# Forgetting attention scored in two products, and every attention score product made 128 rows deep

## The chip, the cores and the metric

The kernel runs on one core of a Trainium2 chip. TensorE (PE) multiplies matrices; its weight loads (PEld) are counted apart and can overlap the products. VectorE (DVE), ScalarE (ACT) and GpSimd (POOL) do the elementwise work, and SyncE (SP) starts the transfers. The metric is the device time of one execution in microseconds (us); lower is better.

## The reference, cut to what matters

The whole program is two transformer blocks in a row, in float32, over 512 tokens of 1024 features. The first block has a recurrence, a gating unit, attention over a memory and a feed-forward part; the change does not touch it. The second block has two layers; each mixes four branches of 8 heads of 64 features and then runs a feed-forward part. Two of the scores that the change touches:

```python
# forgetting attention: F is the running sum over tokens of log sigmoid(f_logit + f_bias), one per head
logits = einsum('bqhd,bshd->bhqs', q, k) * scale + Fq[..., None] - F[:, :, None, :]
p = softmax(where(causal, logits, neg)); out = einsum('bhqs,bshd->bqhd', p, v)

# selected attention: index scores choose the keys, each query then attends to its best 128
dots  = einsum('bqhd,bsd->bqhs', qi, ki)
score = einsum('bqhs,bqh->bqs', relu(dots), wb * w_scale)
```

Selected attention (after rotary embedding, one key head for 8 query heads) and sliding-window attention (rotary, two key heads, window 128) score queries against keys in the same way. The fourth branch, retention, has score products of its own, which stay as they are.

## The kernel before, in words

All float32 products are made from exact two-part splits: a value is a high part (type fp32r) plus a low part, and a weight product `psmm` runs three products per 128 features: high by high (L189), high by low (L190), low by high (L191). Each weight tile is loaded by SP, cast to its high part by ACT (L167), and its low part is made by POOL in this block (`sub`, L112). Three weight tiles of each part are held (`wp`, 3 buffers), and four PSUM banks for these products.

In block 2, `mix2` writes the work of a layer in this order: the rotary keys and index queries, the small natural parts `msc`, the selection (`select`), the sums' rows of the forgetting heads (`fox_rows`), then four forgetting pairs, four pairs of selected attention, the first branch's gates and products, the sliding windows, and so on. Attention itself is written as Python generators (`attend`). `pump(rate)` advances the first generator of a background list by that many steps between weight products, so that softmax work stands between weight products; `drain` runs one to its end. `select` sits in a second list, one step a pump: 3 steps of index scores, 8 steps of two rounds of maxima on DVE (`max`, `match_replace`), then the masks. A scheduler then orders each engine's instructions from this program order and its own model, and places tiles in free slots. A slot of 2 KiB a partition is taken with `g()`; there are 52 of them.

`attend` handles two heads (one pair) over four chunks of 128 queries. For each chunk and head it takes a PSUM bank (three of them, shared with the transposes), calls `score`, reduces the bank with the mask on DVE (L968), exponentiates on ACT (L124), scales on DVE (L982), and one chunk later transposes the probabilities (L995), copies them out (ACT, L998) and multiplies by the values (L1003), which takes 128 rows by 64 columns of the array. Causal chunks have 128, 256, 384 and 512 keys; sliding windows have 128 and then 256.

The score of a head needs the 64 features of q and k in high and low parts. For rotary heads, `stack_q` puts q's high part in one half of the partitions and its low part in the other, and `stack_k` holds the keys' high parts in both halves (`hh`) and the low parts in both halves (`ll`). L1089 multiplies all 128 rows of q by `hh`; L1090 multiplies the 64 rows of q's high part by the same rows of `ll`. The index scores of `select` do the same in L1106 and L1108. For forgetting heads, `fox_pair` builds a pair from the projections: `q` and `kk` per head, `kl` for both. L1074 is the 128-row product, L1075 the 64-row one with the keys' low parts, and L1077 a third with 4 rows, which adds `F_q - F_s` from the rows that `fox_rows` left in `fq` and `fk`: 128 partitions for four heads, each head's sums in the first four rows of a quarter, zeros in the rest.

Of the kernel before, what the change touches and what calls it, by code (L numbers as in the profile page):

```python
# [9 lines left out]
F32 = mybir.dt.float32  # L10
# [7 lines left out]
P = 128  # L18
# [27 lines left out]
# columns of the vector table  # L46
# [13 lines left out]
# columns of the constant table  # L60
# [11 lines left out]
class Builder:  # L72
# [14 lines left out]
    # ---- small helpers  # L87
# [8 lines left out]
    def g(self, dt=F32, n=None):  # L96
        """A slot of 2 KiB a partition that lives long."""
        x = self.gp.tile([P, S], dt, name=self.nm("g"), tag="g", bufs=NSLOT)
        return x if n is None else x[:, :n]
# [34 lines left out]
    def cload(self, name, i=0, long=False):  # L134
        """A constant of the table, brought in for a while."""
        x = self.g() if long else self.tmp()
        a = CST[name][0] + i * S
        self.nc.sync.dma_start(x, self.I["cst"][:, a:a + S])
        return x
# [23 lines left out]
    # ---- exact two-part splits  # L163
# [29 lines left out]
    def gemm_b(self, ps, w, x, start=True, stop=True, off=0):  # L193
        """out^T [features, tokens] += w^T x, w: (hi, lo) [P, len(x)*P], x: list of (hi, lo) tiles."""
        hi, lo = w
        for k, (xh, xl) in enumerate(x):
            a = off + k * P
            self.mm3(ps, hi[:, a:a + P], lo[:, a:a + P], xh, xl,
                     start and k == 0, stop and k == len(x) - 1)

    def gemm_a(self, src, x, ncol, units, ntok=S):
        """natural [tokens, ncol]: one bank per 128 tokens; src[u] is [P, kts*ncol]."""
# [14 lines left out]
    # ---- norms  # L217
    def rms_prep(self, xs, gname, n, gain=None):
        """Split x*g into hi/lo tiles; returns them with a call that leaves the per-token
        factors (row, column), to be made once a product has been set off."""  # L220
# [13 lines left out]
    def square_sum(self, acc, x, k, g=None):  # L234
        """acc += (x*g)^2, tile k of the features"""
# [21 lines left out]
    def to_row(self, rc, n):  # L257
        """[tokens, 1] columns to a row, the same on every partition."""
# [10 lines left out]
    # ---- the whole program  # L269
# [31 lines left out]
    # ================= block 1  # L301
    def mix1(self):
        nc, I = self.nc, self.I
        self.rate, self.lo_every = 1, LO_MIX1
        # the recurrence's inputs, by way of DRAM into blocks of 8 tokens
# [35 lines left out]
        # spatial gating  # L341
# [74 lines left out]
        # gated linear unit after the recurrence, then its projection  # L416
# [60 lines left out]
    def cmul(self, outr, outi, ar, ai, br, bi, shape, eng=None, neg_im=False):  # L477
        """Complex product; with neg_im, outi is minus the imaginary part."""
# [17 lines left out]
    def s5(self, xa_d):  # L496
        """Both directions of the recurrence, in 64 blocks of 8 tokens; partitions of the
        states: (direction, state). Leaves gelu(y), features on partitions, in self.ys5."""
# [10 lines left out]
        # powers of exp(lam * step)  # L509
# [23 lines left out]
        # b_bar = (lam_bar - 1) / lam * b  # L533
# [14 lines left out]
        # powers by position in a block: into the block's end state, and out of it  # L548
# [14 lines left out]
        # block inputs: [(s, c), g, j]  # L563
# [15 lines left out]
        # end-of-block states of each block alone  # L579
# [34 lines left out]
        # the recurrence over blocks  # L614
# [11 lines left out]
    def s5_out(self):  # L626
# [9 lines left out]
        for q in range(4):  # L636
            if q % 2 == 0:
# [36 lines left out]
                # lags -7..7 in DRAM; row s of the block reads lags -s..7-s  # L674
# [31 lines left out]
        # back to features on partitions: [(q, g, c) of one half, tokens]  # L706
# [42 lines left out]
    def xhead(self, h, q, o):  # L749
        """Softmax attention of one head over the memory."""  # L750
# [78 lines left out]
    def final1(self):  # L829
        """The norm that ends block 1 and the one that begins block 2, in one: products run on  # L830
        x*g1*g2, unscaled; the residual goes to DRAM."""
# [28 lines left out]
    # ================= block 2  # L860
# [16 lines left out]
    def finish(self, src, off, hs):  # L877
        """The last products, the last residual and the norm of the output, by token halves."""
# [36 lines left out]
    # ---- rotary embedding; a bank holds two heads, each as its two halves  # L915
# [15 lines left out]
    def stack_q(self, o):  # L931
        """A tile of each of two heads: high parts beside their 64 rows' low parts."""
# [7 lines left out]
    def stack_k(self, o):  # L940
        """Of each of two heads, the high parts twice and the low parts twice."""
# [9 lines left out]
    # ---- softmax attention of two heads over query chunks  # L951
    def attend(self, ys, pair, score, mask, init, value, blocks, sinks=None):
        """Generator; leaves the split output tile [2 heads x 64, tokens] in ys[pair]."""
# [59 lines left out]
    def fox_bias(self, l, msc):  # L1013
        """Running sums of log sigmoid(f + b), as rows for a product that adds F_q - F_s."""
# [12 lines left out]
    def fox_rows(self, f):  # L1027
# [3 lines left out]
        for hg in range(2):  # L1031
            # each head's sums in four rows of a quarter of the partitions
# [22 lines left out]
    def fox_pair(self, ys, pair, pq, pk, va):  # L1055
# [4 lines left out]
        q, kk, kl = [self.g(F32R) for _ in range(2)], [self.g(F32R) for _ in range(2)], self.g(F32R)  # L1060
        for i in range(2):
            r, o = slice(i * 64, i * 64 + 64), slice(64 - i * 64, 128 - i * 64)
            nc.scalar.copy(kk[i][r], tk[r])
            nc.scalar.copy(kk[i][o], tk[r])
            self.sub(kl[r], tk[r], kk[i][r].bitcast(F32))
            nc.scalar.copy(q[i][r], tq[r])
            self.sub(q[i][o], tq[r], q[i][r].bitcast(F32))

        def score(i, c, ps, k0, nk):
            r = slice(i * 64, i * 64 + 64)  # L1070
            h = 2 * pair + i
            qs = slice(c * P, (c + 1) * P)
            mm = nc.tensor.matmul
            mm(ps, q[i][:, qs], kk[i][:, k0:k0 + nk], start=True, stop=False)  # L1074
            mm(ps, q[i][r, qs], kl[r, k0:k0 + nk], start=False, stop=False)  # L1075
            r = slice(h % 4 * 32, h % 4 * 32 + 4)
            mm(ps, self.fq[h // 4][r, qs], self.fk[h // 4][r, k0:k0 + nk], start=False, stop=True)  # L1077
# [5 lines left out]
    def rope_pair(self, ys, pair, q, hh, ll, mask, init, value, blocks, sinks=None):  # L1083
        nc = self.nc

        def score(i, c, ps, k0, nk):
            qs = slice(c * P, (c + 1) * P)
            r = slice(i * 64, i * 64 + 64)
            nc.tensor.matmul(ps, q[i][:, qs], hh[:, k0:k0 + nk], start=True, stop=False)  # L1089
            nc.tensor.matmul(ps, q[i][r, qs], ll[r, k0:k0 + nk], start=False, stop=True)  # L1090
# [3 lines left out]
    def select(self, si, hh, ll, msc):  # L1094
        """Additive masks that leave the 128 best causal keys of each query."""
# [4 lines left out]
        for c in range(1, CHUNKS):  # L1100
            nk = (c + 1) * P
            sc = self.g(F32, nk)
            for h in range(4):
                ps = self.bank("sc")
                r = slice(h % 2 * 64, h % 2 * 64 + 64)
                nc.tensor.matmul(ps[:, :nk], si[h][:, c * P:(c + 1) * P], hh[:, :nk],  # L1106
                                 start=True, stop=False)
                nc.tensor.matmul(ps[:, :nk], si[h][r, c * P:(c + 1) * P], ll[r, :nk],  # L1108
                                 start=False, stop=True)
# [24 lines left out]
    def retain(self, ys, q, k, vc, sg):  # L1134
        """Retention and its head norm, chunk by chunk; q, k: four tiles [2 heads x 64, tokens]."""
# [10 lines left out]
        for c in range(CHUNKS):  # L1146
# [51 lines left out]
            # sums of each head for its norm  # L1198
# [37 lines left out]
    def branch(self, l, n, y, x, first, gens=(), lead=3):  # L1236
        """merged += 2 sigmoid(gate) * (y @ w_branch); the gates run ahead of the products
        with y, which gens may still be working on."""
# [29 lines left out]
    def out_proj(self, src, xd, m=None, scale=0.5, late=0):  # L1268
        """x += scale * (m @ w); merged, where no m is given, holds twice its value. The last
        tiles of m, late of them, may still be under way in the background."""  # L1270
# [29 lines left out]
    def mix2(self, l):  # L1300
# [16 lines left out]
        # keys of the single heads, the index queries, the small natural parts  # L1317
# [6 lines left out]
        # forgetting attention  # L1324
# [14 lines left out]
        # selected attention  # L1339
# [12 lines left out]
        # sliding windows  # L1352
# [16 lines left out]
        # retention  # L1369
# [80 lines left out]
# ---- the host: layout only  # L1450
def _pack_b(w, cols=None):
    """[K, N] -> [N/128, 128, K] blocks: stationary tiles of one output tile, all K."""
# [8 lines left out]
def _pack_b2(w):  # L1461
    """As _pack_b for K = 512, two output tiles to a unit."""
# [5 lines left out]
def _pack_a(w, cols, units):  # L1468
    """[K, N] -> [units, 128, K/128/units * N]: moving rows."""
# [45 lines left out]
def _layout(a):  # L1515
# [30 lines left out]
    # features of the recurrence as the kernel holds them: (half, quarter, group of four, channel)  # L1546
# [50 lines left out]
```

## Time and profile before

| | |
|---|---|
| median of 3 runs | 3202.38 us (3199.94 to 3208.05) |
| span of the profiled execution, first to last instruction | 3194.7 us |
| median less span | 7.7 us |
| TensorE busy | 98% of the span, 14986 products |
| weight loads, DVE, ACT, POOL busy | 79%, 59%, 42%, 30% |
| mean granted TensorE clock | 0.991 |

The page gives a span for the execution that was profiled and no other time of its own; what lies around the span is taken as the 7.7 us to the median. In rows of the trace, "128*128" is rows by columns of the array that a product or load uses, followed by the partitions and columns of what it streams; times are microseconds from the span's start. The ends of matmuls are modelled, so the step from one start to the next is read here and not their length.

### The profile page before, as it was taken

What the parts mean: (1) busy time and instruction counts of PE and PEld (TensorE: products, weight loads), DVE (VectorE), ACT (ScalarE), POOL (GpSimd) and SP (SyncE); (2) the same over time, 40 slices, a digit from 0 to 9 for tenths busy, and PEclk for the clock granted to TensorE, in tenths of its full rate; (3) what the DMA queues carried; (4) which work ended last, traced back from release to release, by engine and by line L of the source; (5) the groups of instructions that cost most, each with busy time, mean ns of one, the idle gap of its engine ahead of it and who ended that gap; (6) DMA issues with size and microseconds to landing.
All of it is one profiled execution on the core that took longest, in us unless ns stands there. A gap on an engine that the chain in (4) does not pass through costs nothing.

```text
span 3194.7 us, 39292 instructions
## 1 busy us (share of the span) xinstructions
PE 3122.7 (98%) x14986; PEld 2508.8 (79%) x14986; DVE 1876.0 (59%) x3423; ACT 1332.8 (42%) x2230; POOL 966.8 (30%) x578
## 2 busy tenths in 40 slices
PE   8998999999998999999999999999999999999998
PEld 6877878888887776777888888877777778888887
DVE  7898554455447685444456666548645454565575
ACT  5523343322225455545234333355455352343343
POOL 4234242211005332344454000053232545610011
PEclk9999999999999999999999999999999999999999
DMA  4224342323323211122223323332111222323322
GB/s 157 75 77 107 91 158 93 99 89 97 106 84 112 83 66 40 64 72 80 76 86 119 99 92 101 96 121 67 60 53 53 83 80 75 119 94 99 96 92 83
DMA packets 98076, 287.12 MB, mean 90 GB/s; under 512 B 11984, under 2 KB 20432, under 8 KB 97888
## 3 DMA queue, kind: packets, MB, share of 16 engines
q1 hardware_dynamic: 97888, 284.61, 27.9%
q8 instruction: 118, 1.93, 0.2%
q14 instruction: 70, 0.57, 0.1%
HBM read 274.64 MB, written 9.93 MB: 89 GB/s over the span
## 4 chain that ended last, share of the span: by engine, by line
PE 89%; DVE 6%; issue 2%; DMA 1%; POOL 1%; ACT 1%; SPq 0%; DVEq 0%; POOLq 0%; ACTq 0%
PE psmm L189 25%; PE psmm L191 25%; PE psmm L190 25%; PE pspv L1003 2%; DVE tmp L112 2%; PE pssc L995 2%; PE pssc L1090 1%; PE pssc L1089 1%; PE pssc L1075 1%; PE pssc L1077 1%; DVE tmp L1215 1%; DVE g L112 1%; PE pssc L1074 1%; POOL lo L112 1%; DVE s5t L112 0%
## 5 line engine op out<-in xcount | busy, mean ns | idle before, releaser
L191 PE MATMUL psmm<-g,lo 128*128 128x512 f32 (+1 forms) x3456 | 1350.3, 391 | 4.0 <-POOL lo L112 4.0
L189 PE MATMUL psmm<-g,hi 128*128 128x512 f32 (+1 forms) x3456 | 1350.7, 393 | 2.2 <-ACT g L167 1.3
L190 PE MATMUL psmm<-g,hi 128*128 128x512 f32 (+1 forms) x3456 | 1349.7, 391 | 1.4 <-DVE g L171 1.4
L112 POOL TENSOR_TENSOR lo<-raw,hi 128x1024 fp32r<-128x1024 f32 (+1 forms) x259 | 632.1, 2442 | 1101.1 <-ACT hi L167 949.0
L167 ACT CAST hi<-raw 128x1024 fp32r<-128x1024 f32 (+3 forms) x506 | 507.7, 1005 | 1080.7 <-PE psmm L190 761.2
L191 PEld LDWEIGHTS psmm<-g,lo 128*128 128x128 f32 x3456 | 650.5, 188 | 143.0 <-POOL lo L112 5.3
L189 PEld LDWEIGHTS psmm<-g,hi 128*128 128x128 f32 x3456 | 650.1, 188 | 142.1 <-issue 4.3
L190 PEld LDWEIGHTS psmm<-g,hi 128*128 128x128 f32 x3456 | 651.1, 188 | 133.9 <-issue 4.3
L112 POOL TENSOR_TENSOR tmp<-tmp,tmp 128x512 f32<-128x512 f32 (+1 forms) x121 | 166.8, 1381 | 1018.8 <-DVE tmp L1417 570.7
L112 DVE TENSOR_TENSOR lo<-raw,hi 128x1024 fp32r<-128x1024 f32 (+2 forms) x247 | 298.0, 1207 | 88.6 <-ACT hi L167 88.6
L112 DVE TENSOR_TENSOR tmp<-psmm,g 128x512 f32<-128x512 f32 x236 | 161.6, 688 | 305.5 <-PE psmm L191 253.9
L189 PE MATMUL psmm<-hi,g 128*128 128x512 f32 (+1 forms) x384 | 144.5, 384 | 16.1 <-ACT g L124 10.8
L1443 DVE SCALAR_TENSOR_TENSOR g<-psmm,g 128x512 f32<-128x512 f32 x88 | 60.7, 690 | 152.5 <-PE psmm L191 152.5
L124 ACT ACTIVATE prob<-prob,nmx 128x128 f32<-128x128 f32 (+2 forms) x192 | 102.7, 535 | 113.6 <-DVE nmx L968 112.4
L190 PE MATMUL psmm<-lo,g 128*128 128x512 f32 (+1 forms) x384 | 146.3, 384 | 2.4 <-POOL lo L112 2.4
L191 PE MATMUL psmm<-hi,g 128*128 128x512 f32 (+1 forms) x384 | 145.3, 382 | 0.0
L112 DVE TENSOR_TENSOR g<-tmp,g 64x512 fp32r<-64x512 f32 (+1 forms) x162 | 128.2, 791 | 13.3 <-ACT g L167 11.0
L1417 DVE SCALAR_TENSOR_TENSOR tmp<-tmp,vec,tmp 128x511 f32<-128x511 f32 (+1 forms) x176 | 131.0, 746 | 2.0 <-ACT tmp L124 0.6
L124 ACT ACTIVATE tmp<-tmp 128x512 f32<-128x512 f32 (+1 forms) x138 | 84.1, 613 | 108.9 <-DVE tmp L112 96.7
L998 ACT COPY probT<-pssc 128x128 f32<-128x128 f32 (+2 forms) x192 | 70.5, 399 | 123.7 <-PE pssc L995 117.9
L982 DVE TENSOR_SCALAR prob<-prob,sm 128x128 f32<-128x128 f32 (+2 forms) x192 | 101.0, 568 | 2.5
L189 PEld LDWEIGHTS psmm<-hi,g 128*128 128x128 f32 x384 | 74.6, 195 | 29.4 <-ACT g L124 10.8
(274 smaller groups left out, 3126.1 us busy)
## 6 DMA issues: line engine op xcount, KB each, us to landing
raw<-w_up SPq DMA_DIRECT2D x110, 512.0 KB, 3.4
raw<-w_gates SPq DMA_DIRECT2D x64, 512.0 KB, 3.5
raw<-w_down SPq DMA_DIRECT2D x72, 384.0 KB, 3.1
raw<-w_rope SPq DMA_DIRECT2D x40, 512.0 KB, 3.6
raw<-w_branch SPq DMA_DIRECT2D x32, 512.0 KB, 3.4
raw<-w_out SPq DMA_DIRECT2D x24, 512.0 KB, 3.5
raw<-w_gate SPq DMA_DIRECT2D x22, 512.0 KB, 3.6
raw<-w_fox SPq DMA_DIRECT2D x16, 512.0 KB, 3.5
```

What stands on the lines that cost most here:

```text
L112: (eng or self.nc.vector).tensor_tensor(out, a, b, op)
L124: self.nc.scalar.activation(out, in_, func, **k)
L167: nc.scalar.copy(hi, src)
L189: mm(out, sh, mh, start=start, stop=False)
L190: mm(out, sh, ml, start=False, stop=False)
L191: mm(out, sl, mh, start=False, stop=stop)
L982: nc.vector.tensor_scalar(pt[i][:, :nk], pt[i][:, :nk], sm[:, i:i + 1], None, ALU.mult)
L995: nc.tensor.transpose(tr[:, j * P:(j + 1) * P], pt[i][:, j * P:(j + 1) * P], self.ident)
L998: nc.scalar.copy(ptT[:, :n * P], tr[:, :n * P])
L1003: nc.tensor.matmul(pv[i * 64:(i + 1) * 64, pc * P:(pc + 1) * P], value(i, b), tt[i][:, j * P:(j + 1) * P], start=j == 0, stop=j == n - 1)
L1417: nc.vector.scalar_tensor_tensor(o[:, sh:], u[:, :S - sh], w, o[:, sh:], ALU.mult, ALU.add)
L1443: self.nc.vector.scalar_tensor_tensor(self.x[d], ps, 0.5, self.x[d], ALU.mult, ALU.add)
```

## The change: two full products for each score

For rotary and index scores, the second product takes the whole 128-row tile of q and the whole of `ll`, so that low parts of q meet low parts of k as well. For forgetting scores there are now two products of 128 rows. The first is as before. The second has the stationary tile `q2` and the moving tile `k2`, new for each head: q's high parts against the keys' low parts in one half of the rows, and in the other half the 64 rows of `fq` that hold the pair's two heads against `fk` in the 32 rows of this head and zeros in the other head's 32 rows. Comment lines are blank in the changed file as well, and lines behind `fox_pair` move down by up to five.

```diff
-        q, kk, kl = [self.g(F32R) for _ in range(2)], [self.g(F32R) for _ in range(2)], self.g(F32R)
+        q, k = [self.g(F32R) for _ in range(2)], [self.g(F32R) for _ in range(2)]
+        q2, k2 = [self.g(F32R) for _ in range(2)], [self.g(F32R) for _ in range(2)]
+        hg, f0 = pair // 2, pair % 2 * 64
+        fq, fk = self.fq[hg], self.fk[hg]
         for i in range(2):
             r, o = slice(i * 64, i * 64 + 64), slice(64 - i * 64, 128 - i * 64)
-            nc.scalar.copy(kk[i][r], tk[r])
-            nc.scalar.copy(kk[i][o], tk[r])
-            self.sub(kl[r], tk[r], kk[i][r].bitcast(F32))
+            mine, other = 64 - i * 64 + i * 32, 64 - i * 64 + 32 - i * 32
+            nc.scalar.copy(k[i][r], tk[r])
+            nc.scalar.copy(k[i][o], tk[r])
+            self.sub(k2[i][r], tk[r], k[i][r].bitcast(F32))
+            nc.gpsimd.memset(k2[i][other:other + 32].bitcast(F32), 0.0)
+            nc.scalar.copy(k2[i][mine:mine + 32], fk[f0 + i * 32:f0 + i * 32 + 32].bitcast(F32))
             nc.scalar.copy(q[i][r], tq[r])
             self.sub(q[i][o], tq[r], q[i][r].bitcast(F32))
+            nc.scalar.copy(q2[i][r], tq[r])
+            nc.scalar.copy(q2[i][o], fq[f0:f0 + 64].bitcast(F32))
 
         def score(i, c, ps, k0, nk):
-            r = slice(i * 64, i * 64 + 64)
-            h = 2 * pair + i
             qs = slice(c * P, (c + 1) * P)
-            mm = nc.tensor.matmul
-            mm(ps, q[i][:, qs], kk[i][:, k0:k0 + nk], start=True, stop=False)
-            mm(ps, q[i][r, qs], kl[r, k0:k0 + nk], start=False, stop=False)
-            r = slice(h % 4 * 32, h % 4 * 32 + 4)
-            mm(ps, self.fq[h // 4][r, qs], self.fk[h // 4][r, k0:k0 + nk], start=False, stop=True)
+            nc.tensor.matmul(ps, q[i][:, qs], k[i][:, k0:k0 + nk], start=True, stop=False)
+            nc.tensor.matmul(ps, q2[i][:, qs], k2[i][:, k0:k0 + nk], start=False, stop=True)
...
-            r = slice(i * 64, i * 64 + 64)
             nc.tensor.matmul(ps, q[i][:, qs], hh[:, k0:k0 + nk], start=True, stop=False)
-            nc.tensor.matmul(ps, q[i][r, qs], ll[r, k0:k0 + nk], start=False, stop=True)
+            nc.tensor.matmul(ps, q[i][:, qs], ll[:, k0:k0 + nk], start=False, stop=True)
...
-                r = slice(h % 2 * 64, h % 2 * 64 + 64)
-                nc.tensor.matmul(ps[:, :nk], si[h][:, c * P:(c + 1) * P], hh[:, :nk],
-                                 start=True, stop=False)
-                nc.tensor.matmul(ps[:, :nk], si[h][r, c * P:(c + 1) * P], ll[r, :nk],
-                                 start=False, stop=True)
+                qc = si[h][:, c * P:(c + 1) * P]
+                nc.tensor.matmul(ps[:, :nk], qc, hh[:, :nk], start=True, stop=False)
+                nc.tensor.matmul(ps[:, :nk], qc, ll[:, :nk], start=False, stop=True)
```

## The prediction

> **What bounds the kernel now.** I read the page first: busy shares, then the chain that ended last. After that came the timeline of TensorE around single score products, to see what one of them costs, and last the busy time by stretch, to see who else is full there.
>
> ```profile
> span 3194.7 us, 39292 instructions
> PE 3122.7 (98%) x14986; PEld 2508.8 (79%) x14986; DVE 1876.0 (59%) x3423; ACT 1332.8 (42%) x2230; POOL 966.8 (30%) x578
> PE 89%; DVE 6%; issue 2%; DMA 1%; POOL 1%; ACT 1%; SPq 0%; DVEq 0%; POOLq 0%; ACTq 0%
> ```
>
> TensorE is 89% of the chain, so time taken from its queue is time taken from the kernel, unless another engine is about as late at that place. A busy matmul says little, since matmuls overlap; what counts is the step from one start to the next. Here is one score of the rotary kind (256 keys, two products) among plain weight products, then weight products of 256 and of 204 columns:
>
> ```profile
> 1493.80 0.39 PE L191 MATMUL psmm<-g,lo 128*128 128x512 f32 x1
> 1494.03 0.28 PE L1089 MATMUL pssc<-g,g 128*128 128x256 f32 x1
> 1494.23 0.38 PE L1090 MATMUL pssc<-g,g 64*128 64x256 f32 x1
> 1494.55 0.50 PE L189 MATMUL psmm<-g,hi 128*128 128x512 f32 x1
> 1494.88 0.40 PE L190 MATMUL psmm<-g,hi 128*128 128x512 f32 x1
> ```
>
> ```profile
> 345.00 0.28 PE L191 MATMUL psmm<-g,lo 128*128 128x256 f32 x1
> 345.12 0.28 PE L189 MATMUL psmm<-g,hi 128*128 128x256 f32 x1
> ```
>
> ```profile
> 1011.25 0.27 PE L191 MATMUL psmm<-hi,g 128*128 128x204 f32 x1
> 1011.36 0.28 PE L189 MATMUL psmm<-hi,g 128*128 128x204 f32 x1
> ```
>
> The first number is the start. In a run of 128-row products a step is 0.23 us for 512 columns (1493.80 to 1494.03), 0.12 for 256 and 0.11 for 204. I take 0.11 for 128 columns too (0.51 us for two such products, below, is a bound from above) and 0.17 for 384, between 0.12 and 0.23. Around the 64-row product everything is longer: 0.20 before it, 0.32 for it, and 0.33 for the weight product after it, which on its own takes 0.23. The weight loads say why:
>
> ```profile
> 1096.42 0.19 PEld L1074 LDWEIGHTS pssc<-g,g 128*128 128x128 f32 x1
> 1096.79 0.18 PEld L1075 LDWEIGHTS pssc<-g,g 64*128 64x128 f32 x1 [0.18 <-issue]
> ```
>
> L1074's load starts a product ahead of its matmul (1096.64, next fence); the load of the 64-row L1075 starts with its matmul at 1096.79. So a change in the number of rows lengthens the step before it (0.20 instead of 0.12) and leaves the load behind it uncovered (0.33 instead of 0.23), some 0.18 us for each change. The Trainium skill, "TensorEngine Tiling (Array Packing)", section "Key Properties", says that changing the tiling mode drains the TensorE, without a price; the trace agrees, and has the price.
>
> **The change part by part.** *Rotary scores (L1090), 128 of them.* The second product takes all 128 rows, against keys' low parts that already stand twice. Both changes of row count go. The score above takes 1494.03 to 1494.88, that is 0.85 us with its follower, and becomes 0.12 + 0.12 + 0.23 = 0.47: 0.38 saved. For 384 and 512 columns I take the same 0.38, since neither part has a reason to grow with the columns. For 128 columns the step is bound by the load:
>
> ```profile
> 1241.43 0.33 PE L1089 MATMUL pssc<-g,g 128*128 128x128 f32 x1
> 1241.69 0.32 PE L1090 MATMUL pssc<-g,g 64*128 64x128 f32 x1
> 1241.94 0.38 PE L1089 MATMUL pssc<-g,g 128*128 128x256 f32 x1
> ```
>
> 0.51 against 0.22 is 0.29; where a probability-value product (128 rows but 64 columns, a change of its own that stays) follows, less: 0.25. The widths:
>
> ```profile
> L1090 PE MATMUL pssc<-g,g x128: 322/381/502, 1240.8 to 2634.1; 64*128 64x256 f32 x64, 64*128 64x128 f32 x32, 64*128 64x384 f32 x16, 64*128 64x512 f32 x16
> ```
>
> 32 x 0.25 + 96 x 0.38 = 44.5 us. *Index scores (L1106, L1108)*: 3 chunks x 4 heads x 2 layers = 24, of 256 columns and more: 24 x 0.38 = 9.1 us.
>
> *Forgetting scores (L1074, L1075, L1077), 64 of them*, 16 of each width. Three products with 128, 64 and 4 rows make three changes of row count; they become two products without a change. First 128 and 256 columns, then 512:
>
> ```profile
> 1096.64 0.22 PE L1074 MATMUL pssc<-g,g 128*128 128x128 f32 x1
> 1096.79 0.32 PE L1075 MATMUL pssc<-g,g 64*128 64x128 f32 x1
> 1097.05 0.32 PE L1077 MATMUL pssc<-g,g 4*128 4x128 f32 x1
> 1097.30 0.38 PE L1074 MATMUL pssc<-g,g 128*128 128x256 f32 x1
> 1097.61 0.38 PE L1075 MATMUL pssc<-g,g 64*128 64x256 f32 x1
> 1097.92 0.38 PE L1077 MATMUL pssc<-g,g 4*128 4x256 f32 x1
> 1098.23 0.50 PE L189 MATMUL psmm<-g,hi 128*128 128x512 f32 x1
> 1098.57 0.39 PE L190 MATMUL psmm<-g,hi 128*128 128x512 f32 x1
> ```
>
> ```profile
> 1124.81 0.49 PE L1074 MATMUL pssc<-g,g 128*128 128x512 f32 x1
> 1125.23 0.50 PE L1075 MATMUL pssc<-g,g 64*128 64x512 f32 x1
> 1125.66 0.50 PE L1077 MATMUL pssc<-g,g 4*128 4x512 f32 x1
> 1126.09 0.50 PE L191 MATMUL psmm<-g,lo 128*128 128x512 f32 x1
> ```
>
> The first two take 1096.64 to 1098.57 = 1.93 with the follower, and become 0.22 + 0.24 + 0.23 = 0.69: 1.24 saved. The 512 one takes 1.28 and 0.11 in its follower = 1.39; the load before it stays uncovered (a probability-value product precedes it), so it becomes 0.10 + 0.46 = 0.56: 0.83 saved. For 384 columns I take 0.76, between the two. A head's four chunks save 1.24 + 0.76 + 0.83 = 2.83, and 16 heads 45.3 us.
>
> Together 44.5 + 9.1 + 45.3 = 98.9 us of TensorE's queue.
>
> *What stays of it.* Where DVE is full, TensorE cannot get ahead for long, since it waits for the softmax of the chunk before:
>
> ```profile
> 1093.00:1187.00 94.00, 94.00 (x431) 70.31 (x430) 89.28 (x233) 52.13 (x99) 35.95 (x17) 1.00 0.22 73
> 2177.00:2272.00 95.00, 95.00 (x431) 70.75 (x430) 91.87 (x232) 51.73 (x98) 34.83 (x16) 1.00 0.22 72
> ```
>
> The columns are the stretch, its length, and the busy us (and instructions) of TensorE, weight loads, DVE, ACT and POOL; then clock and DMA. In these two stretches the selection's rounds of maxima run beside the forgetting scores, and DVE has 4.7 and 3.1 us free. Each holds 16 of the 64 scores:
>
> ```profile
> 1093.00:1187.00 94.00, 6.53 (x16) 2.90 (x16) 1.00 0.22 73
> 2177.00:2272.00 95.00, 6.51 (x16) 2.90 (x16) 1.00 0.22 72
> ```
>
> (the same stretches, L1077 alone). 16 x 0.71 = 11.3 us are freed in each, DVE lets through 4.7 and 3.1, and 6.6 + 8.2 = 14.8 us are lost. It could be none, if DVE's lateness is carried into the half-empty time behind; it could be all 22.6, if DVE's gaps cannot be closed. I take 14.8.
>
> *Operands of the forgetting heads.* For each of 8 pairs ACT makes 12 copies in place of 6, DVE's subtractions stay 4, POOL gains two memsets.
>
> ```profile
> L1063 ACT CAST g<-tmp x16: 603/616/622, 1083.2 to 2241.0; 64x512 fp32r<-64x512 f32 x16
> L1034 POOL MEMSET tmp<- x4: 524/530/534, 1055.3 to 2152.1; 128x512 f32 x4
> ```
>
> ACT: 48 x 0.616 = 29.6 us in all, 3.7 a pair. POOL: 16 x 0.53 = 8.5 us, behind its low-part subtractions, with 58 of 94 us free in that stretch. ACT is 55% busy there, so its work is covered; but DVE's subtraction now waits behind two or three copies instead of two, where DVE is full. Bounds: nothing, if DVE takes other work meanwhile, to 29.6 us, if DVE stands through all of it. The cover is good (DVE has the selection to do), so I take a small share, 4 us, an estimate. A pair holds 8 slots of 2 KiB in place of 5, but the sums' rows go free once the pairs are built. No DMA is added, moved or removed.
>
> Sum: 98.9 - 14.8 - 4 = 80.1 us. The profiled span is 3194.7, the median of the runs 3202.4, 7.7 us more than the span and untouched: 3202.4 - 80.1 = 3122.
>
> **The rivals.** (a) DVE carries its lateness on and ACT costs nothing: all 98.9 us come through, 3103.5. For it: DVE is only 44% busy behind the first stretch.
>
> ```profile
> 1187.00:1240.00 53.00, 51.80 (x278) 35.64 (x277) 23.09 (x68) 25.73 (x64) 7.12 (x3) 1.00 0.09 31
> ```
>
> Against it: the scores' softmax stands in DVE's queue among the selection's rounds.
>
> (b) DVE waits for ACT's longer row of copies at full price, and the stretches give nothing: 98.9 - 22.6 - 29.6 = 46.7, 3156. Against it: only six of the eight builds lie near a full DVE.
>
> (c) The change does not do what it says: the uncovered load belongs to the score products themselves and not to the change of row count. Then only the third forgetting product goes, 16 x (0.25 + 0.31 + 0.37 + 0.43) = 21.8 us, less 4: 3185. A page speaks for it: the Trainium skill, "TensorE: Matmul & The Clock Gate", section "The mechanism", has a weight load overlap a running matmul only where the row groups differ, so that full-row products would uncover every load. This trace shows the opposite, L1074's load of 128 rows a product ahead at 1096.42.
>
> (d) Slower: ACT stops at a copy into a slot that is not yet free. Three pairs are in building while the first has its last chunk still before it:
>
> ```profile
> 1102.84 0.62 ACT L1064 CAST g<-tmp 64x512 fp32r<-64x512 f32 x1
> ```
>
> ```profile
> 1126.43 0.40 PE L1074 MATMUL pssc<-g,g 128*128 128x512 f32 x1
> ```
>
> At 8 slots each, beside some 28 long-lived ones (by the allocations in the code), three pairs are all 52. If my count is two short, the third build holds ACT, and behind it the weights' high parts, from 1102.8 to 1126.4, 24 us; if the fourth waits alike, that is 96 us over both layers: 3122 + 96 = 3218. It decides from 80 us on, so both waits must stand nearly in full. Against it: when the fourth pair is built the first pair's slots are free, and three weight tiles in advance, 24 products of 0.23 us each, cover some 16 us of a wait.
>
> **How the numbers follow.** My forecast, 3110 to 3136, has a chance of 0.50; (a) 0.25; (b), in whole or most part, 0.18; (c) 0.05; (d) 0.02. The range leaves out (c) and (d) and the far end of (b): from 3096 (all freed, and some us of reordering) to 3152. Of this kernel 0.3%, 10 us, is about what can be told from no change; (c) is faster too, by 0.5%. Faster 0.95, same 0.03 (a part of (d)), slower 0.02.
>
> **What the profile after would show.** No score product with fewer than 128 rows; TensorE 64 products fewer (14922); steps of 0.11, 0.12 and 0.23 us between score products, and their loads a product ahead. In the two full stretches DVE at 98% or more and short waits of TensorE for DVE. ACT about 30 us busier, POOL 8. The prediction is wrong if full-row scores still take 0.3 us a step, if TensorE waits for ACT's copies, or if the stretches shrink by 11 us each.

## The result, and the profile after

The changed kernel takes 3117.23 us (median of 4 runs, 3113.99 to 3118.62) against 3201.16 us before on the same chip: a ratio of 0.9731, 95% interval 0.9713 to 0.9749. It is 83.9 us faster; forecast were 80, and 3122 us.

The page of the changed kernel, its span, busy shares and chain:

```profile
span 3116.7 us, 39233 instructions
PE 3031.5 (97%) x14922; PEld 2481.6 (80%) x14922; DVE 1884.2 (60%) x3423; ACT 1352.9 (43%) x2278; POOL 974.6 (31%) x594
PE 82%; DVE 11%; ACT 2%; DMA 2%; issue 2%; POOL 1%; SPq 0%; DVEq 0%; ACTq 0%; POOLq 0%
```

TensorE has the 64 products fewer that were forecast, ACT 48 instructions and POOL 16 more. TensorE's share of the chain falls from 89% to 82%, and DVE's rises from 6% to 11%. The spans differ by 78.0 us and the medians by 83.9. This profiled execution took 3118.62 us, 1.9 us more than its span. So the 7.7 us between span and median before were probably for the most part an execution faster than the median, and not time outside the span.

A rotary score of 256 keys after the change, first the products and then the weight loads in the timeline:

```profile
1457.15 0.39 PE L191 MATMUL psmm<-g,lo 128*128 128x512 f32 x1
1457.38 0.28 PE L1093 MATMUL pssc<-g,g 128*128 128x256 f32 x1
1457.49 0.28 PE L1094 MATMUL pssc<-g,g 128*128 128x256 f32 x1
1457.61 0.40 PE L189 MATMUL psmm<-g,hi 128*128 128x512 f32 x1
1457.84 0.40 PE L190 MATMUL psmm<-g,hi 128*128 128x512 f32 x1
```

```profile
1457.15 0.19 PEld L1093 LDWEIGHTS pssc<-g,g 128*128 128x128 f32 x1
1457.38 0.19 PEld L1094 LDWEIGHTS pssc<-g,g 128*128 128x128 f32 x1
1457.49 0.19 PEld L189 LDWEIGHTS psmm<-g,hi 128*128 128x128 f32 x1
```

The steps are 0.11, 0.12 and 0.23, and every load starts a product ahead of its matmul. The score with its follower takes 1457.38 to 1457.84 = 0.46 us, where it took 0.85. The forgetting score of 512 keys, behind a probability-value product:

```profile
1171.54 0.43 PE L1003 MATMUL pspv<-probT,h 128*64 128x128 f32 x2
1171.90 0.50 PE L1081 MATMUL pssc<-g,g 128*128 128x512 f32 x1
1172.23 0.39 PE L1082 MATMUL pssc<-g,g 128*128 128x512 f32 x1
1172.46 0.40 PE L191 MATMUL psmm<-g,lo 128*128 128x512 f32 x1
```

0.33 with the load that stays uncovered, then 0.23: 0.56, as worked out.

**Where the time came from.** Two landmarks cut a layer: the last product that makes the forgetting sums (L1040), and the first and last probability-value product with the values `msc`, which both rotary branches use (L1003). Each row ends its times with the first and last start. Before, first and second layer:

```profile
L1040 PE MATMUL pssc<-tmp,tmp x16: 273/432/591, 1064.7 to 1076.7; 128*128 128x512 f32 x4, 128*128 128x384 f32 x4, 128*128 128x256 f32 x4, 128*128 128x128 f32 x4
L1003 PE MATMUL pspv<-probT,msc x272: 272/273/324, 1247.4 to 1557.5; 128*64 128x128 f32 x136
L1040 PE MATMUL pssc<-tmp,tmp x16: 272/432/591, 2149.5 to 2161.5; 128*128 128x512 f32 x4, 128*128 128x384 f32 x4, 128*128 128x256 f32 x4, 128*128 128x128 f32 x4
L1003 PE MATMUL pspv<-probT,msc x272: 272/273/324, 2339.7 to 2649.8; 128*64 128x128 f32 x136
```

After:

```profile
L1040 PE MATMUL pssc<-tmp,tmp x16: 272/432/592, 1063.0 to 1075.0; 128*128 128x512 f32 x4, 128*128 128x384 f32 x4, 128*128 128x256 f32 x4, 128*128 128x128 f32 x4
L1003 PE MATMUL pspv<-probT,msc x272: 272/273/325, 1227.5 to 1517.4; 128*64 128x128 f32 x136
L1040 PE MATMUL pssc<-tmp,tmp x16: 273/432/591, 2109.5 to 2121.4; 128*128 128x512 f32 x4, 128*128 128x384 f32 x4, 128*128 128x256 f32 x4, 128*128 128x128 f32 x4
L1003 PE MATMUL pspv<-probT,msc x272: 272/273/325, 2281.7 to 2571.7; 128*64 128x128 f32 x136
```

| part of a layer | before | after | saved |
|---|---|---|---|
| forgetting part, L1040's last to `msc`'s first, layer 1 | 170.7 | 152.5 | 18.2 |
| the same, layer 2 | 178.2 | 160.3 | 17.9 |
| rotary part, `msc`'s first to last, layer 1 | 310.1 | 289.9 | 20.2 |
| the same, layer 2 | 310.1 | 290.0 | 20.1 |

That is 76.4 us of the 78.0. The forgetting part holds the stretch where DVE is full: it ends where the selection's last replacement starts (`match_replace`, L1126 before and L1128 after). The two pieces of the forgetting part before the change, first and then second layer (columns as in the prediction):

```profile
1076.70:1183.70 107.00, 106.93 (x477) 79.27 (x475) 101.21 (x247) 60.60 (x112) 39.30 (x18) 1.00 0.21 70
1183.70:1247.40 63.70, 62.50 (x332) 42.44 (x332) 30.55 (x96) 31.51 (x81) 7.12 (x3) 1.00 0.09 32
2161.50:2270.90 109.40, 109.40 (x487) 80.37 (x486) 104.31 (x249) 60.36 (x111) 39.60 (x18) 1.00 0.22 71
2270.90:2339.70 68.80, 67.16 (x344) 46.34 (x342) 32.91 (x95) 32.60 (x82) 9.52 (x4) 0.98 0.10 31
```

After:

```profile
1075.00:1181.30 106.30, 101.64 (x496) 80.61 (x495) 104.07 (x253) 74.60 (x139) 43.84 (x26) 1.00 0.24 75
1181.30:1227.50 46.20, 44.67 (x284) 33.14 (x282) 26.73 (x90) 28.95 (x78) 7.12 (x3) 1.00 0.11 35
2121.40:2231.20 109.80, 103.57 (x502) 82.49 (x501) 106.52 (x245) 75.41 (x137) 46.90 (x27) 1.00 0.24 76
2231.20:2281.70 50.50, 47.69 (x297) 35.54 (x295) 30.34 (x98) 29.79 (x80) 7.19 (x3) 1.00 0.10 32
```

The full stretch keeps its length (107.0 and 106.3 us, 109.4 and 109.8). DVE has about as much to do in it, and is now 98% and 97% busy (95% before). TensorE was never free there before, and now is not busy for 4.7 and 6.2 us. Yet it starts more products there, 496 and 502 in place of 477 and 487, though 15 and 16 of those before were third products of forgetting scores. It gets ahead with other work, and this work is missing behind the stretch, where the time is saved: 63.7 becomes 46.2 us, and 68.8 becomes 50.5.

### The profile page after: what moved, and what is told of

Read it like the earlier page. It is cut to its first block, busy times and chain, and to the rows that moved or that the text cites. A ratio compares the mean times of both kernels' runs of the same rounds, so it can differ in the third digit from the quotient of the medians.

```text
span 3116.7 us, 39233 instructions
## 1 busy us (share of the span) xinstructions
PE 3031.5 (97%) x14922; PEld 2481.6 (80%) x14922; DVE 1884.2 (60%) x3423; ACT 1352.9 (43%) x2278; POOL 974.6 (31%) x594
## 3 DMA queue, kind: packets, MB, share of 16 engines
q1 hardware_dynamic: 97888, 284.61, 29.6%
## 4 chain that ended last, share of the span: by engine, by line
PE 82%; DVE 11%; ACT 2%; DMA 2%; issue 2%; POOL 1%; SPq 0%; DVEq 0%; ACTq 0%; POOLq 0%
PE psmm L189 24%; PE psmm L190 24%; PE psmm L191 24%; DVE tmp L112 3%; PE pspv L1003 2%; DVE g L112 2%; PE pssc L995 1%; DVE g L1128 1%; DVE m L1127 1%; PE pssc L1093 1%; DVE tmp L1217 1%; PE pssc L1094 1%; DVE s5t L112 0%; PE pspv L791 0%; PE pssc L759 0%
## 5 line engine op out<-in xcount | busy, mean ns | idle before, releaser
L982 DVE TENSOR_SCALAR prob<-prob,sm 128x128 f32<-128x128 f32 (+2 forms) x192 | 93.2, 527 | 2.5
```

What stands on the lines that cost most here:

```text
L982: nc.vector.tensor_scalar(pt[i][:, :nk], pt[i][:, :nk], sm[:, i:i + 1], None, ALU.mult)
```

## The experiments

Each run was timed against the kernel before on its own chip, whose median lay between 3196 and 3201 us. Where two experiments are compared, the lengths of the two parts above say more than the medians.

**One half of the change each.** First only rotary and index scores:

```diff
-            nc.tensor.matmul(ps, q[i][r, qs], ll[r, k0:k0 + nk], start=False, stop=True)
+            nc.tensor.matmul(ps, q[i][:, qs], ll[:, k0:k0 + nk], start=False, stop=True)
```

> Rotary and index scores have full-row products as in the change; forgetting scores stay as they were (three products of 128, 64 and 4 rows, old operands). Theory (the price hangs on each change of the number of rows, TensorE is the bound in the rotary stretches): 44.5 + 9.1 us freed, some 2 us of the index scores' share lost to the full DVE behind them, so about 52 us faster than before: 3149 us. Rival (rotary stretches have another bound as well): half of it, 3175 us. Rival (the price belongs to score products as such): no change, 3201 us.

Measured: 3149.3 us, ratio 0.9844 (0.983 to 0.9858), 49.1 us faster than 3198.4. Then only the forgetting scores (`fox_pair` of the changed file in the kernel before):

> Only the forgetting scores are changed (two full products, new operands); rotary and index scores keep their 64-row second product. Theory (DVE is full beside half of these scores): 45.3 - 14.8 - 4 = 26.5 us faster than before, 3175 us. Rival (DVE's lateness is carried on and nothing is lost): 45 us faster, 3156 us. Rival (the operands' ACT copies are paid in full): 45.3 - 22.6 - 29.6, about 3208 us.

Measured: 3168.9 us, ratio 0.9906 (0.9893 to 0.992), 29.5 us. The halves add up to 78.6 us, close to the whole. The theory's numbers held within 6 us in both, and the rivals lie 13 us and more away. The lengths of the parts (in the table at the end of this section) are more careful. The rotary half saves 40.2 us in the rotary parts and 2.3 in the forgetting parts, 42.5 of the 53.6 freed by forecast. Another 4.5 us of its shorter span lie before the first landmark, which stands anywhere from 1071.7 to 1079.0 us in the runs and has only four index scores in front of it, so the median flatters this half. The forgetting half saves 29.9 us in the forgetting parts, of the 45.3 freed by forecast.

**The number of products, and the operands.** Two runs keep the old operands (6 copies, no memset, 5 slots) and differ only in the score:

```diff
             mm(ps, q[i][:, qs], kk[i][:, k0:k0 + nk], start=True, stop=False)
-            mm(ps, q[i][r, qs], kl[r, k0:k0 + nk], start=False, stop=False)
-            mm(ps, self.fq[h // 4][r, qs], self.fk[h // 4][r, k0:k0 + nk], start=False, stop=True)
+            mm(ps, q[i][:, qs], kl[:, k0:k0 + nk], start=False, stop=False)
+            mm(ps, self.fq[h // 4][:, qs], self.fk[h // 4][:, k0:k0 + nk], start=False, stop=True) 
```

> As the change, but forgetting scores have three products, all of 128 rows, made from the old operands (6 ACT copies a pair, no memset, 5 slots); the keys' low parts and the sums' rows of other heads are not masked out, so the scores hold terms that do not belong there. Theory: the third product costs its plain step, 64 x 0.16 = 10 us of TensorE, half of it beside the full DVE where it costs nothing; against that the operands' 4 us go: 3117 + 5 - 4 = 3118 us. Rival (the number of products is what counts, 0.34 us each): 3117 + 22 = 3139 us.

> As the change, with two full products for forgetting scores, but from the old operands (6 ACT copies a pair, no memset, 5 slots); the forgetting sums are left out of the scores. Theory (operands cost little): 4 us less than the changed kernel, 3113 us. Rival (ACT's longer row of copies is paid in full): 3088 us. Rival (it is all covered): 3117 us.

Measured: 3127.2 us with three products (0.9776, 0.9763 to 0.979), 3126.3 us with two (0.9778, 0.9765 to 0.9792). The third product of full rows costs 1 us, where 5 were expected and a price per product would be 22. (TensorE is busy 6.5 us longer with it in the two forgetting parts; its waits are shorter by as much. The `diff` shows the run with three; the one with two leaves out its last line.) So it is the rows, and not the smaller number of products, that make the forgetting half faster.

But both are 9 to 10 us slower than the change itself, with fewer copies, where I expected 1 us more for the first and 4 us less for the second. The rotary part says that nothing is lost there (1232.7 to 1522.7 = 290.0):

```profile
L1040 PE MATMUL pssc<-tmp,tmp x16: 272/432/591, 1059.8 to 1071.7; 128*128 128x512 f32 x4, 128*128 128x384 f32 x4, 128*128 128x256 f32 x4, 128*128 128x128 f32 x4
L1003 PE MATMUL pspv<-probT,msc x272: 272/273/324, 1232.7 to 1522.7; 128*64 128x128 f32 x136
```

The first layer's forgetting part takes 161.0 us here and 152.5 in the changed kernel; the second's 160.7 (2125.6 to 2286.3) and 160.3. The difference stands in one layer, and 6.2 of its 8.5 us in the full stretch. The second layer is as long with the change's ACT copies as without them, so they have no price there that shows.

Why the first layer is longer can in part be read in the traces. DVE's 341 instructions of that part keep it busy for 138.3 us here and for 130.8 in the changed kernel. The maxima take the same time in both. But some subtractions and scalings take 2 us and more where others of the same shape take 0.69 or less, and those stand beside a GpSimd instruction. Two subtractions of DVE in the changed kernel, and GpSimd's work beside the second (two instructions in one row):

```profile
1109.62 0.69 DVE L112 TENSOR_TENSOR g<-tmp,g 64x512 fp32r<-64x512 f32 x1
1112.18 2.12 DVE L112 TENSOR_TENSOR g<-tmp,g 64x512 fp32r<-64x512 f32 x1
1111.37 5.19 POOL L112 TENSOR_TENSOR lo<-raw,hi 128x1024 fp32r<-128x1024 f32 x2 [3.90 <-DMA raw<-w_rope]
```

In the forgetting parts of the twelve kernels in the table below, 299 DVE instructions take over 0.15 us more than the lower quartile of their kind, and all of them overlap with a GpSimd instruction. In the first layer the excess adds up to 18.2 us here and to 9.9 in the changed kernel. So it seems that the order in which the scheduler places DVE's work also sets how long this work takes. TensorE's longest wait in that layer is 4.2 us here and 1.2 in the changed kernel, and its mean granted clock 0.98 and 1.00. No run changed the order alone, so how much of the 8.5 us each of these makes is not shown.

**Is DVE the bound of that stretch?** Half of the selection is left out, in the changed kernel and in the one before:

```diff
-        for r in range(16):
+        for r in range(8):
```

> The changed kernel with 8 rounds of maxima in the selection in place of 16, so the masks keep half as many keys; DVE has some 28 us less to do in each layer's full stretch. Theory (DVE's fullness there holds back about 15 us of the freed time): the stretches become TensorE's again and some 13 to 18 us come back, about 3102 us. Rival (the stretches lose their share to something else: ACT's copies, slots): no change, 3117 us.

> The kernel before, with the same 8 rounds of maxima in place of 16. Theory (before the change TensorE is the bound even there): within 3 us of the kernel before, 3199 us. Rival (DVE held the stretch back before the change as well): as much as in the changed kernel, 3185 us.

Measured: 3107.1 us after the change (3105.3 to 3108.6; ratio 0.9711, 0.9692 to 0.973), 10 us less than with the whole selection; 3196.9 us before it (0.9989, 0.9977 to 1.0), no clear difference. The stretch after the change with the whole selection and with half of it, then before the change with half:

```profile
1075.00:1177.00 102.00, 97.34 (x474) 77.10 (x473) 99.90 (x243) 73.61 (x136) 43.84 (x26) 1.00 0.23 73
1074.00:1177.00 103.00, 102.01 (x530) 81.97 (x529) 86.57 (x189) 78.68 (x148) 43.86 (x26) 1.00 0.25 77
1073.00:1176.00 103.00, 102.93 (x463) 75.66 (x462) 79.92 (x185) 61.31 (x115) 37.09 (x17) 1.00 0.23 72
```

With DVE at 84%, TensorE starts 530 products in 103 us instead of 474 in 102. Before the change, taking the same work from DVE buys nothing: 463 products in 103 us, with TensorE full. The forgetting parts say the same: 172.2 and 177.4 us before with half a selection, 146.9 and 156.4 after, so 46.3 us saved, against 36.1 with the whole selection:

```profile
L1040 PE MATMUL pssc<-tmp,tmp x16: 272/432/591, 1062.3 to 1074.3; 128*128 128x512 f32 x4, 128*128 128x384 f32 x4, 128*128 128x256 f32 x4, 128*128 128x128 f32 x4
L1003 PE MATMUL pspv<-probT,msc x272: 272/273/324, 1221.2 to 1511.1; 128*64 128x128 f32 x136
```

The difference is 10 us, 7.1 in the first layer and 3.1 in the second; between the medians it is 6 (the change saves 89.8 us with half a selection, 83.9 with the whole). That DVE's rounds hold TensorE back after the change, and did not before it, is shown by the two pairs of runs. The size is less certain, since half a selection also changes the order on DVE. TensorE's own idle time in the two forgetting parts tells it another way: 2.9 us before the change and 15.2 after it, 1.9 and 9.3 with half the selection.

**Giving DVE less to do without leaving anything out.** The four subtractions of a pair's build go to GpSimd:

```diff
-            self.sub(k2[i][r], tk[r], k[i][r].bitcast(F32))
+            self.sub(k2[i][r], tk[r], k[i][r].bitcast(F32), nc.gpsimd)
-            self.sub(q[i][o], tq[r], q[i][r].bitcast(F32))
+            self.sub(q[i][o], tq[r], q[i][r].bitcast(F32), nc.gpsimd)
```

> The changed kernel with the four subtractions of a forgetting pair's build on GpSimd in place of DVE, 24 us of DVE's work over both layers, most of it in the full stretches. Theory: the stretches get shorter by a part of it, 5 to 12 us, about 3109 us. Rival (GpSimd's queue, where the weights' low parts stand in order, makes the builds late): 3117 us or more.

Measured: 3122.4 us (0.976, 0.9741 to 0.9779), 5 us slower than the change and so against the theory. GpSimd's groups from 1075 to 1180:

```profile
L112 POOL TENSOR_TENSOR lo<-raw,hi 128x1024 fp32r<-128x1024 f32 x14 | 33.6, 2402 | 32.7 <-ACT hi L167 32.0 <-PE pssc L1082 0.4 <-POOL g L1072 0.2
L112 POOL TENSOR_TENSOR g<-tmp,g 64x512 fp32r<-64x512 f32 x16 | 21.7, 1355 | 3.8 <-ACT g L1074 2.4 <-ACT g L1069 0.5
```

The moved subtractions take 1.36 us each there. The selection ended earlier (its last replacement starts at 1168.7), and TensorE waited elsewhere in the part; which of the builds was late was not settled. DVE's busy time in the two forgetting parts falls by 12.3 us only, where the moved instructions took 24: with more work on GpSimd, the excess of DVE instructions beside it grows from 25.5 to 35.7 us.

**Slots.** `NSLOT = 48` in place of 52.

> The changed kernel with 48 slots of 2 KiB in place of 52. If three pairs in building need all 52 slots, as counted in the prediction, the third build now waits for the first pair's last score and ACT stands in front of it: 10 to 40 us slower, about 3140 us. If the count has slack, 3117 us.

Measured: 3127.3 us (0.9774, 0.9754 to 0.9793), 10 us slower, the lower end of what was expected. But no row of ACT standing in front of a copy appears: the third pair's copies start 22.7 us after the first pair's with 48 slots (1103.7) and 20.1 us after them with 52 (1101.1), and ACT works in between. The count is not refuted, and the mechanism of rival (d) is not shown.

**The price of a change of rows by itself.** Far from any score, in the feed-forward part, half of the features are left out of one product, or of two neighbours, of each of the 88 up-projection tiles:

```python
        for k, (xh, xl) in enumerate(x):
            a = k * P
            n = 64 if k == 4 else P
            m = 64 if k == 4 and 1 == 2 else P  # 2 == 2 in the run with two
            mm(ps, hi[:m, a:a + P], xh[:m], start=k == 0, stop=False)
            mm(ps, hi[:n, a:a + P], xl[:n], start=False, stop=False)
            mm(ps, lo[:, a:a + P], xh, start=False, stop=k == len(x) - 1)
```

> The changed kernel with one of the 24 products of each of the 88 up-projection tiles of block 2's feed-forward part (far from any score) cut to 64 rows, so that half of its features are left out of that product. Theory (the price belongs to each change of the number of rows): two changes a tile, 0.09 before it, 0.20 for it and 0.11 behind it, 0.40 us x 88 = 35 us slower than the changed kernel, 3152 us. Rival (the price belongs to the score products, not to the rows): 3117 us.

> The same with two neighbouring products of each tile cut to the same 64 rows. Theory (per change): the number of changes stays two, 3152 us. Rival (each product of fewer rows pays for its own load): 0.20 us x 88 = 18 us more, 3170 us.

Measured: 3151.3 us (0.9859, 0.9845 to 0.9872) and 3153.8 us (0.9863, 0.985 to 0.9877). 34 us more than the changed kernel for one, 37 for two, or 0.39 and 0.42 us a tile (taken from each run's ratio to the kernel before, 41 and 42 us). The second product adds 3 us at most, not 18, and the steps in the traces give 0.39 a tile for one and for two. With two:

```profile
1685.56 0.39 PE L211 MATMUL psmm<-g,lo 128*128 128x512 f32 x1
1685.88 0.49 PE L209 MATMUL psmm<-g,hi 64*128 64x512 f32 x1
1686.21 0.39 PE L210 MATMUL psmm<-g,hi 64*128 64x512 f32 x1
1686.53 0.50 PE L211 MATMUL psmm<-g,lo 128*128 128x512 f32 x1
1686.87 0.40 PE L209 MATMUL psmm<-g,hi 128*128 128x512 f32 x1
```

Between the two 64-row products the step is 0.33, 0.10 above the plain 0.23, and all of it is the first one's uncovered load; the second's load is covered. The product before the change has 0.32 and the one behind the second change 0.34. Four extras of about 0.1, two for each change. The price belongs to the change of the number of rows, and rival (c) is out. The Trainium skill, "TensorE: Matmul & The Clock Gate", section "The mechanism", has one sentence that lets a load overlap a running product only where the row groups differ, and another that also lets it go ahead into a background weight buffer. Here, and in the loads of L1094 above, a load is covered where the rows stay the same and uncovered where they change, so the measurement decides against the first; the second fits.

**Moving the selection later.** One round a step in place of two beside the forgetting scores, the rest before the first branch:

```diff
-            if r % 2:
-                yield
+            yield
...
-            if j == 0:
-                self.drain(sel)
+            self.rate2 = 2
...
+        self.drain(sel)
+        self.rate2 = 1
         self.branch(l, 0, ya, x, True, ga, LEAD[0])
```

> The changed kernel with all 16 rounds of the selection, but one round a step in place of two beside the forgetting scores, two steps a pump in the stretch of the next four projections, and the rest before the first branch, so that some 20 us a layer of DVE's work move from the full stretch to the emptier one behind it. Theory (what is lost is lost to a DVE that is full too early): most of the 10 us that half a selection gave come back, 3109 us. Rival (the moved rounds hold up the next pairs' softmax in the same way): 3117 us or more.

Measured: 3116.1 us (0.9745, 0.9732 to 0.9759). The edit did not do what it was for: the selection's last maximum starts at 1175.4 (1177.3 in the changed kernel, which reaches L1040 1.9 us later as well), and both parts of both layers have the lengths of the changed kernel within 0.1 us. The scheduler, it seems, places the rounds wherever its model has DVE free, however they are spread in the program. So the last run holds them by data as well:

```diff
+                if r == 6:
+                    nc.vector.scalar_tensor_tensor(sc[:, 0:1], self.hook[:, 0:1], 0.0, sc[:, 0:1], ALU.mult, ALU.add)
...
+            if j == 3:
+                self.hook = o  # the fourth rotary projection
```

> As the run before (selection spread), and the seventh round of maxima now reads one column of the fourth rotary projection behind the forgetting pairs (times zero), so that 10 of the 16 rounds cannot run before it; in the run before, the order on DVE had hardly moved. Theory (what is lost is lost to a DVE that is full too early): the forgetting scores' softmax comes earlier, the rounds end near the first rotary score, and 4 to 8 of the 10 us that half a selection gave come back, 3111 us. Rival (the total of DVE's work up to the first rotary score counts, not its place): 3117 us. Rival (the rounds end too late for the rotary scores): 3122 us or more.

Measured: 3122.9 us (0.9756, 0.9742 to 0.9769), slower than the change. Busy time by slices (columns as before):

```profile
1120.00:1140.00 20.00, 19.63 (x106) 14.95 (x105) 13.98 (x36) 14.81 (x29) 12.11 (x7) 1.00 0.20 62
1140.00:1160.00 20.00, 20.00 (x100) 15.81 (x100) 19.70 (x53) 15.77 (x30) 7.17 (x5) 1.00 0.22 74
1160.00:1180.00 20.00, 19.47 (x104) 14.98 (x104) 19.81 (x46) 8.98 (x16) 5.97 (x4) 1.00 0.17 54
1180.00:1200.00 20.00, 14.66 (x72) 11.08 (x71) 19.78 (x56) 8.22 (x18) 4.68 (x2) 0.85 0.26 79
```

TensorE's longest wait of this layer, and the last 5 us of these slices:

```profile
1193.39 0.50 PE L191 MATMUL psmm<-g,hi 128*128 128x512 f32 x1 [3.92 <-DVE g L113]
1195.00:1200.00 5.00, 3.58 (x9) 2.31 (x9) 4.78 (x10) 0.63 (x1) 0.44 (x1) 0.50 0.36 105
```

DVE now has room at 1120 to 1140 and is full up to 1200 instead, where TensorE is free for 5.3 of 20 us. The full stretch has moved with the rounds: a weight product stands for 3.9 us behind a subtraction of DVE in it, and the granted clock is 0.50 behind that wait. The theory of a DVE that is only full too early falls. The time is that of the last rival (3122 us or more), but its mechanism is not seen: the last replacement starts at 1191.5, and the first rotary score at 1229.1. That only DVE's whole work up to there counts fits half the selection, but not this run (3117 us by that rival; the first layer's part is 6 us longer, the second's unchanged), and not the subtractions on GpSimd, which took 12 us from DVE and made it slower.

The lengths of the two parts in these runs, first and second layer, read at the same landmarks:

| run | forgetting part | rotary part |
|---|---|---|
| before | 170.7, 178.2 | 310.1, 310.1 |
| changed | 152.5, 160.3 | 289.9, 290.0 |
| rotary only | 168.6, 178.0 | 290.0, 290.0 |
| forgetting only | 154.4, 164.6 | 310.1, 310.1 |
| three full / two full, old operands | 159.4, 162.2 / 161.0, 160.7 | 290.0, 289.9 / 290.0, 290.0 |
| half selection, changed / before | 146.9, 156.4 / 172.2, 177.4 | 289.9, 289.9 / 310.0, 310.1 |
| subtractions on GpSimd | 160.9, 158.1 | 289.9, 290.0 |
| 48 slots | 161.7, 162.7 | 290.1, 290.0 |
| selection spread / held | 152.5, 160.3 / 158.8, 160.0 | 289.9, 289.9 / 290.0, 290.0 |

The rotary part has two lengths and no others, with full rows and without. In the first layer the forgetting part takes 152.5 to 161.0 us in versions whose TensorE has the same number of products there (776 to 778), so by 8.5 us more or less. This is not noise between executions: it is 152.5 again in the selection spread, whose order hardly moved, and in both runs of the feed-forward experiment, which leave this part alone. The changed kernel is at the short end; five other versions that keep both halves and the whole selection need 158.8 to 161.7 us there (of these, three full products have 32 products more, and 48 slots 19). No version was found that beats the changed kernel; the one with the selection spread has its lengths and a median 1.1 us lower, which is no difference.

## Why the prediction was right

**The price of a change of rows** (0.18 us, of which 0.08 to 0.09 before and 0.10 behind) was right. It was read from one score and came back as 0.39 us for two changes in a place without scores (0.40 was expected there), and did not grow with a second 64-row product.

**Rotary scores**: forecast 44.5 us, measured 20.2 + 20.1 = 40.3 in the rotary part. Six scores of each layer start before the landmark; counted from the first rotary score (1240.5 and 2332.8 before, 1221.8 and 2276.1 after), each layer saves 21.4, 42.8 in all. The term is thus about 2 us too large. Its samples were scores with a weight product behind them; scores followed by a probability-value product keep that change, and I took this off for 128 columns only.

**Forgetting and index scores**: forecast 45.3 + 9.1 us freed. Of the index scores, 8 of 12 a layer fall into the forgetting part, 6.1 us, and the early rotary scores another 2.5. TensorE's busy time in the two forgetting parts fell by 48.4 us (345.99 to 297.57 in the rows above), where these terms make 54; with half the selection the parts get 46.3 us shorter, with TensorE still waiting for 9.3.

**What DVE holds back**: forecast 14.8, measured about 10 (46.3 less 36.1), or 12.3 by TensorE's added idle time. The place was right: the stretch with the selection went to DVE. The mechanism was right in half. The prediction had DVE let through its free time of 4.7 and 3.1 us, with TensorE unable to get ahead for long. In fact the stretch is no shorter (0.7 us less and 0.4 more), TensorE does get ahead in it, and what it did ahead is saved behind it. So lateness was carried on in part, as rival (a) had it in full.

**The operands**: forecast 4 us, measured none that can be told from the scatter of the forgetting part. ACT grew by 20.1 us of busy time and POOL by 7.8, where 29.6 and 8.5 were counted; rival (b), which paid the copies in full, is out.

**The sum** came out at 80.1 against 78.0 between the two profiled spans. The rotary part gave 4.2 us less than its term. The forgetting part was to give 51.4 less 18.8, 32.6 us, and gave 36.1. These two nearly cancel, and that is luck. It is also luck that the scheduler gave the changed kernel a good order: the versions around it, with as many products, needed 6 to 9 us more in the first layer. Between the medians it is 83.9; the 5.9 us beside the spans are mostly the profiled execution before, which ran faster than the median, and not anything in the sum. The 7.7 us that the prediction took as untouched time around the span were of the same kind. The chance of 0.50 was put on 3110 to 3136, which holds the result.

Five theories of the experiments missed. The two runs with old operands were 9 us slower than the changed kernel where 1 us more and 4 us less were expected; moving work off DVE, spreading the selection and holding it were to help and did not. All had the same wrong picture, in which the amount of DVE's work sets the forgetting part. Its order is worth as much as the term itself, and my sum had no range for that.

## What to carry to other kernels

Look at the steps from start to start around products with fewer rows, not at their length: on this TensorE a lone 64-row product among 128-row ones cost about 0.4 us beyond its own step, and filling the rows, even with terms that add nothing, was nearly free. When a bound engine gets faster in a stretch where the next engine is nearly full, the stretch may keep its length and the gain show up behind it. The order of the next engine's queue can move the result by as much as the estimate itself. Here a scheduler's order did not move when the work was only written elsewhere, and moved when data held it.

## What the runs showed of the hardware that was not expected

Two neighbouring products on the same 64 rows cover each other's loads like full ones: the second step is 0.32 and not the 0.43 of a single one. A DVE subtraction or scaling can take 2 us in place of 0.7 beside a GpSimd instruction, while the maxima beside one keep their time; so DVE's busy time depends on what GpSimd does. And a wait of TensorE for DVE can cost clock as well: behind the wait of 3.9 us above the granted clock was 0.50 for a slice. The changed kernel, whose longest wait in these parts was 2.2 us, was granted 1.00 in all four pieces; but in the run with subtractions on GpSimd the clock of the first part was 0.97, with no wait over 2.6 us. No length of wait that decides it was found.
